# A two-layer hybrid trunk: the mixer's tiles in two pools, stores issued by ScalarE, another first order of gate and up

## The chip, the cores and the metric

The kernel runs on one core of one Trainium2 chip. The metric is the device time of one execution in microseconds (us). Before the change it is 2234.05 us, the median of 3 runs (2232.53 to 2235.14). TensorE (PE) multiplies, VectorE (DVE), ScalarE (ACT) and GpSimd (POOL) work on tiles, SyncE (SP) issues most of the loads. Each engine takes its own instructions in order; a DMA is issued by an engine and then runs beside it.

## The reference

Two layers of a transformer-like trunk on 256 tokens of width 2048, all in float32. Cut to what matters here:

```python
for l in range(2):
    h = rms_norm(x, pre_mix_norm[l])
    m = hybrid_mixer(h, ...)            # h @ w_in, two kinds of attention, @ w_o
    x = x + rms_norm(m, post_mix_norm[l])
    h = rms_norm(x, pre_ffn_norm[l])
    f = (silu(h @ w_gate[l]) * (h @ w_up[l])) @ w_down[l]      # 2048 -> 5632 -> 2048
    x = x + rms_norm(f, post_ffn_norm[l])
```

The mixer has 8 heads of stick-breaking attention and 8 of differential attention; each head's output is normed, and all are multiplied by `w_o`.

## The kernel before, in words

**Weights.** All weights pass through the core once, in the order that `weight_order` (L49) writes out, as tiles of 256 rows x 512 columns, stored as 128 partitions x 2 x 512 (512 KB). A tile's number is its place in that order. Of a layer's 392 tiles 96 belong to `w_in`, 32 to `w_o`, 176 to gate and up, taken in turn, and 88 to `w_down`. Gate and up of layer 0 begin at tile 128. `kp` (0 to 7) counts the pairs of 128 rows, `c` (0 to 10) the chunks of 512 columns of gate and up.

Each ordinary tile is loaded by SP into `raw` (`fetch`, L150, with the load in L165; four buffers), and split in two parts for the fp32r multiplier: ScalarE writes the rounded `hi`, VectorE the rest `lo = raw - hi` (`feed`, L202; L212 and L214 in the profile; six buffers each). Each product is three matmuls, hi x hi, lo x hi and hi x lo (`product`, L750; L754 to L756 in gate and up, L397 to L399 in the projections). `weights(i, ahead)` lets loads and splits run `LOOKAHEAD` tiles ahead of the matmuls.

**Combined products.** For some `kp` (`sevens`) the 2 x 2 block product of two token halves and the gate and up tiles is made with seven products in place of eight (`seven`, L871, `seven_products`, L771). That needs, besides the gate tile, the sum of up and gate. `summed` (L170) makes it without an engine's arithmetic: SP loads the up tile into `T` (L173), then POOL issues a second DMA that adds the first half of the gate tile to it (L174). The gate tile itself comes as `G` (L161). `fetch` issues `T` up to `EARLY` = 4 tiles ahead of its turn. `mixed_weights` (L179) then splits `T` into `hi` and `lo` (L188 and L189), forms three more tiles from `T` and `G`, and splits these into `Th` and `Tl`. At the end of the last combined `kp` of a chunk, `shared_part` (L788) reads four banks and writes four tiles `w`, with VectorE's last steps in L794 and L795; these release TensorE's banks. The token sums for a combined `kp` (`pair_sums`, L854) are made by VectorE and ScalarE ahead of their use.

In chunk 0 of each layer the order of `kp` is `FIRST_ORDER` (L38), the combined ones are `FIRST_SEVEN` = (4, 6), and `FORM_AT` (L39) says at which place in the order, counted after the first two, which `kp` gets its token sums. In the other chunks the order is 0 to 7 and the combined ones are 2, 4, 5 and 6. So in chunk 0 of layer 0 tiles 128 to 135 are `kp` 0, 1, 3 and 2; before the change 136 and 137 are `kp` 4, the first combined one (`G136`, `T137`).

**Pools.** Every pool is a stretch of on-chip memory, tiles of one `tag` share a ring of buffers, and a new tile waits until the tiles whose room it takes are no longer used. The mixer's tiles (`x`, `mix`, `t2`, `qk`, `v`, `gpost`, the attention weights, `ra`, `rb`) lie in one pool `att{l}` (L800) in the order of their first use. After the mixer it is released, and the FFN's pools `ffn{l}` (L847) and `gu{l}` (L848; `G` with 3 buffers, `T` with 4, `Th`, `Tl`) take the same stretch. The tag `t2` is also that of the squares that the FFN's norm throws away (`inv_rms`, L356). `mix{l}_{k}`, the mixer's normed output, has 16 buffers, made at the start of the layer and written by `norm_pair` (L434).

**From the mixer to the FFN.** Around the last chunk of `w_o` ScalarE's and VectorE's order is written out by hand (`tc.manual_schedule`). `rescale` (L417) adds the normed output to `x`, `transposed` (L330) turns `x` into `xF`, the stationary tiles of the FFN, with ScalarE (L338) and VectorE (L343), `inv_rms` computes the norm's factors for both halves of the tokens, and `put_away` (L245) stores the four quarters of `x` (512 KB each) to DRAM, from which they come back at the end of the FFN. It is called three times: after the mixer of each layer, and at the end of layer 0's FFN, twelve stores in all. Before the change POOL issues them (L250).

The compiler's scheduler places the instructions of each engine; DMAs are tracked by a limited number of completion semaphores (lanes), which the queues of an engine's kind take in turn, so that an issue may have to wait until an earlier transfer on its lane has landed.

Of the kernel before, what the change touches and what calls it, by code (L numbers as in the profile page):

```python
# [9 lines left out]
F32 = mybir.dt.float32  # L10
F32R = mybir.dt.float32r
# [6 lines left out]
P = 128  # L18
D = 2048
S = 256  # L20
L = 2
NT = S // P
KT = D // P
NH = 8
# [10 lines left out]
KP_O = (4, 5, 6, 7, 0, 1, 2, 3)  # L35
SEVEN = (2, 4, 5, 6)
FIRST_SEVEN = (4, 6)
FIRST_ORDER = (0, 1, 3, 2, 4, 5, 6, 7)  # L38
FORM_AT = {1: 4, 3: 6, 4: 5, 5: 2}  # L39
DOWN_SEVEN = (3, 6, 9, 12, 15, 18)  # L40

WARM = 13
# [9 lines left out]
def weight_order():  # L52

    order = []

    def queue_pair(name, l, kp, c):
        order.append((name, l, kp, c))
        return len(order) - 1

    plan = []  # L60
    sevens = set()
    for l in range(L):
        lay = {"in": {}, "o": {}, "gate": {}, "up": {}, "down": {}}
        chunks = []
        for g in range(2):
            chunks += [6 + g, 8 + g, 10 + g]
        for g in range(2):
            chunks += [g, 2 + g, 4 + g]
        lay["chunks"] = chunks
        for c in chunks:  # L70
            for kp in range(KT // 2):
                lay["in"][c, kp] = queue_pair("w_in", l, kp, c)
        order_o = [(c, kp) for kp in KP_O for c in (0, 1)]
        order_o += [(c, kp) for c in (2, 3) for kp in range(KT // 2)]
        lay["order_o"] = order_o
        for c, kp in order_o:
            lay["o"][c, kp] = queue_pair("w_o", l, kp, c)
        for c in range(FF // CW):
            for kp in FIRST_ORDER if c == 0 else range(KT // 2):
                lay["gate"][c, kp] = queue_pair("w_gate", l, kp, c)  # L80
                lay["up"][c, kp] = queue_pair("w_up", l, kp, c)
                if kp in (FIRST_SEVEN if c == 0 else SEVEN):
                    sevens.add(lay["up"][c, kp])
        for half in range(2):
            for kp in range(FF // P // 2):
                for c in (2 * half, 2 * half + 1):
                    lay["down"][c, kp] = queue_pair("w_down", l, kp, c)
                if kp in DOWN_SEVEN:
                    sevens.add(lay["down"][2 * half + 1, kp])
        plan.append(lay)  # L90
    return order, plan, sevens


def weights_laid_out(inputs):

    import numpy as np

    order = weight_order()[0]
    out = np.empty((len(order), P, 2 * CW), np.float32)
    for o, (name, l, kp, c) in zip(out, order):  # L100
        w = inputs[name][l, kp * 2 * P : (kp + 1) * 2 * P, c * CW : (c + 1) * CW]
        o[...] = w.reshape(2, P, CW).transpose(1, 0, 2).reshape(P, 2 * CW)
    return out


@with_exitstack
def kernel(
# [15 lines left out]
    nc = tc.nc  # L123
# [8 lines left out]
    def bank(name):  # L132
        return ps.tile([P, CW], F32, tag="b", bufs=3, name=name)
# [84 lines left out]
    def in_turn():  # L218

        return tc.issue_after(loads[-1].ins)  # L220
# [10 lines left out]
    xs = []  # L231
# [3 lines left out]
    away = []  # L235
# [9 lines left out]
    def put_away(nm):  # L245

        away.append(kept.tile([P, NT, D], F32, name=f"away_{nm}"))
        for t in range(NT):
            for h in range(2):
                nc.gpsimd.dma_start(away[-1][:, t, h * D // 2 : (h + 1) * D // 2], xs[t][h])  # L250

    x_pool = [None]

# [63 lines left out]
    def rsqrt(dst, src, inv, nm):  # L317
        n = dst.shape[-1]
        m = small.tile([P, 2, 4], F32, tag="rsq", bufs=4, name=f"rsq_{nm}")
        u, ms = m[:, 0, 0:n], m[:, 1, 0:n]  # L320
        nc.scalar.activation(u, src, AF.Ln, scale=inv, bias=eps)
        nc.scalar.activation(dst, u, AF.Exp, scale=-0.5)
        nc.vector.tensor_scalar(out=ms, in0=src, scalar1=inv, scalar2=EPS, op0=ALU.mult, op1=ALU.add)
        nc.vector.tensor_tensor(out=u, in0=dst, in1=dst, op=ALU.mult)
        nc.vector.tensor_tensor(out=u, in0=u, in1=ms, op=ALU.mult)
        nc.vector.tensor_scalar(out=u, in0=u, scalar1=-0.5, scalar2=1.5, op0=ALU.mult, op1=ALU.add)
        nc.vector.tensor_tensor(out=dst, in0=dst, in1=u, op=ALU.mult)
# [106 lines left out]
    def norm_pair(pool, ob, mix, mixed, h0, gcol, nm):  # L434
        ss = small.tile([P, 4], F32, tag="oss", name=f"oss_{nm}")
        for i in range(4):
            junk = pool.tile([P, CW], F32, tag="t2", name=f"jo_{nm}_{i}")
            nc.scalar.activation(junk[:, 0:P], ob[:, i * P : (i + 1) * P], AF.Square, accum_out=ss[:, i : i + 1])
        yield
        rs = small.tile([P, 4], F32, tag="ors", name=f"ors_{nm}")  # L440
        rsqrt(rs, ss, 1.0 / P, nm)
        on = pool.tile([P, 4, P], F32, tag="t2", name=f"on_{nm}")
        nc.vector.tensor_tensor(
            out=on, in0=ob.rearrange("p (i d) -> p i d", i=4), in1=rs.unsqueeze(2).to_broadcast([P, 4, P]), op=ALU.mult
        )
        yield
        yield
        pb = bank(f"oT_ps_{nm}")
        for i in range(4):
            nc.tensor.transpose(pb[:, i * P : (i + 1) * P], on[:, i, :], ident)  # L450
        for j in range(2):
            nc.scalar.activation(
                mix[h0 + j][:, 0, :], pb[:, j * S : (j + 1) * S], AF.Copy, scale=gains[:, gcol + j : gcol + j + 1]
            )
            nc.vector.scalar_tensor_tensor(
                out=mix[h0 + j][:, 1, :],
                in0=pb[:, j * S : (j + 1) * S],
                scalar=gains[:, gcol + j : gcol + j + 1],
                in1=mix[h0 + j][:, 0, :].bitcast(F32),
                op0=ALU.mult,  # L460
                op1=ALU.subtract,
            )
            mixed.add(h0 + j)
# [141 lines left out]

    def rotate(pool, tok, t, nm):
        v16 = tok.rearrange("p (h d) -> p h d", d=64)[:, :, 0:16]
        ra = pool.tile([P, NH, 16], F32, tag="ra", bufs=2, name=f"ra_{nm}")
        rb = pool.tile([P, NH, 16], F32, tag="rb", bufs=2, name=f"rb_{nm}")

        def table(a, b):
            return rope_sb[:, t, a:b].unsqueeze(1).to_broadcast([P, NH, b - a])

        eng = nc.gpsimd
        eng.tensor_tensor(out=ra, in0=v16, in1=table(0, 16), op=ALU.mult)
        eng.tensor_tensor(out=rb[:, :, 0:8], in0=v16[:, :, 8:16], in1=table(16, 24), op=ALU.mult)
        eng.tensor_tensor(out=rb[:, :, 8:16], in0=v16[:, :, 0:8], in1=table(24, 32), op=ALU.mult)
        eng.tensor_tensor(out=v16, in0=ra, in1=rb, op=ALU.add)
# [123 lines left out]
            else:  # L742
                evac()

    def load_gain(pool, v, nm):
        gp = pool.tile([P, D], F32, tag="gpost", bufs=1, name=f"gpost_{nm}")
        with in_turn():
            nc.sync.dma_start(gp, v.partition_broadcast(P))
        return gp
# [47 lines left out]
    xT = None  # L797
    for l in range(L):

        pool = tc.alloc_tile_pool(name=f"att{l}", bufs=6, reuse_waits="tile")  # L800
        if l == 0:
            xT = x_tiles("xT0")
            rs = []
        xs[:] = [[pool.tile([P, D // 2], F32, tag="x", bufs=4, name=f"x{l}_{t}_{h}") for h in range(2)] for t in range(NT)]
        mix = [pool.tile([P, 2, S], F32R, tag="mix", bufs=KT, name=f"mix{l}_{k}") for k in range(KT)]
        mixed = set()
        mixer_in(pool, l, rs, xT, mix, mixed)

        gpost = load_gain(pool, post_mix_norm[l], f"mix{l}")
        mg = {}  # L810
        ssm = [small.tile([P, 4], F32, tag="ssm", name=f"ssm_o{l}_{t}") for t in range(NT)]
        accs = {(c, t): acc_bank(f"o{l}_{c}_{t}") for c in (0, 1) for t in range(NT)}
# [34 lines left out]
        pool = tc.alloc_tile_pool(name=f"ffn{l}", bufs=5, reuse_waits="tile")  # L847
# [6 lines left out]
        def pair_sums(kp):  # L854
            f = pool.tile([P, 2, S], F32, tag="t2", name=f"f{l}_{kp}")
            for kk in range(2):
                st = xT[2 * kp + kk]
                nc.vector.tensor_tensor(out=f[:, kk, :], in0=st[:, 0, :].bitcast(F32), in1=st[:, 1, :].bitcast(F32), op=ALU.add)
            forms[kp] = token_sums(pool, gu, len(SEVEN), f[:, 0, 0:P], f[:, 1, 0:P], f[:, 0, P:S], f[:, 1, P:S], f"{l}_{kp}")
# [18 lines left out]
        for c in range(FF // CW):  # L878
            banks = four_banks(c % 2, [f"c{q}_{l}_{c}" for q in ("11", "12", "21", "22")])
            mine = FIRST_SEVEN if c == 0 else SEVEN  # L880
            order = FIRST_ORDER if c == 0 else tuple(range(KT // 2))
            if c == 0:
# [5 lines left out]
            for n, kp in enumerate(order):  # L888
                if c == 0 and n in FORM_AT:
                    pair_sums(FORM_AT[n])  # L890
                if kp not in mine:
# [32 lines left out]
        gpost = load_gain(dn, post_ffn_norm[l], f"ffn{l}")  # L924
# [151 lines left out]
```

## Time and profile before

| | |
|---|---|
| median of 3 runs | 2234.05 us (2232.53 to 2235.14) |
| the profiled execution's own time | 2232.69 us |
| its span, first to last instruction | 2230.9 us |
| PE granted clock, mean | 0.994 |
| DMA | 464.65 MB, mean 208 GB/s |
| SP's `raw` loads, issue to landing, median | 4.3 us |
| POOL's additions into `T`, the same | 6.7 us |
| POOL's stores `away_ffn`, the same | 3.7 us |

A row of the timeline has the start, the length in us, the engine, the line, the operation and its tiles; the bracket at its end holds the idle time of that engine just before and what ended it. Matmul ends are modelled, so the pace of matmuls is read from their starts. PE, PEld (its weight loads), DVE, ACT and POOL are the engines; SPq, POOLq and ACTq are the issues of DMAs. A row "DMA" in the chain is the transfer itself, from issue to landing. The granted clock is the share of TensorE's full speed in a stretch.

### The profile page before, as it was taken

How to read it: one execution, taken by the hardware profiler on the slowest of the kernel's cores; microseconds unless marked ns; L12 is line 12 of the kernel's file. 1: busy time of each engine (PE TensorE's matmuls, PEld its weight loads, DVE VectorE, ACT ScalarE, POOL GpSimd, SP SyncE). 2: the span in 40 equal slices, each digit the busy share in tenths (PEclk: the TensorE clock that was granted, in tenths of full speed). 3: DMA queues.
4: the chain of work that ended last, by engine and by line, in shares of the span. 5: the costliest groups of instructions: out<-in, count | busy, mean ns of one | idle time of the engine just before them, and what ended most of it. 6: DMA issues, size and time to landing. Idle time of an engine off the chain costs nothing.

```text
span 2230.9 us, 28481 instructions
## 1 busy us (share of the span) xinstructions
PE 2197.5 (99%) x10057; PEld 1805.2 (81%) x10057; DVE 1789.6 (80%) x2531; ACT 1308.2 (59%) x1937; POOL 139.8 (6%) x196
## 2 busy tenths in 40 slices
PE   9999999899999999999999999998999999999998
PEld 7888888688888888788877888887888888888886
DVE  6666555799999998989776665557999999999897
ACT  6555554656656656656565455546566566566663
POOL 1100000100000000000020000001000000000000
PEclk9999999999999999999999999999999999999999
DMA  8555555677776675767465554557767767757673
GB/s 289 190 168 163 160 189 183 224 228 233 217 253 213 218 249 184 239 214 241 153 224 171 179 189 160 183 187 229 248 215 225 242 212 228 239 194 245 198 254 100
DMA packets 136784, 464.65 MB, mean 208 GB/s; under 512 B 15681, under 2 KB 16193, under 8 KB 136129
## 3 DMA queue, kind: packets, MB, share of 16 engines
q1 hardware_dynamic: 119216, 428.20, 55.7%
q0 software_dynamic: 17280, 34.61, 8.5%
q8 instruction: 79, 1.29, 0.2%
q14 instruction: 65, 0.52, 0.1%
q10 hardware_dynamic: 144, 0.02, 0.0%
HBM read 454.38 MB, written 8.39 MB: 207 GB/s over the span
## 4 chain that ended last, share of the span: by engine, by line
PE 92%; DMA 3%; ACT 2%; DVE 2%; issue 1%; POOL 0%; SPq 0%; DVEq 0%; ACTq 0%; POOLq 0%
PE c L754 9%; PE c L756 9%; PE c L755 9%; PE in L397 7%; PE in L399 7%; PE in L398 7%; PE dn L960 5%; PE dn L963 5%; PE dn L961 5%; PE o L399 2%; PE o L398 2%; PE o L397 2%; PE p L754 2%; PE p L756 2%; PE p L755 2%; DMA raw<-in_weights_in_turn_dram 2%
## 5 line engine op out<-in xcount | busy, mean ns | idle before, releaser
L214 DVE TENSOR_TENSOR lo<-raw,hi 128x1024 fp32r<-128x1024 f32 x567 | 688.3, 1225 | 237.5 <-ACT hi L212 233.7
L212 ACT ACTIVATE hi<-raw 128x1024 fp32r<-128x1024 f32 x567 | 592.4, 1056 | 389.8 <-PE in L399 167.3
L754 PE MATMUL c<-hi,xF 128*128 128x512 f32 x820 | 324.3, 397 | 1.9 <-DVE w L795 1.6
L756 PE MATMUL c<-hi,xF 128*128 128x512 f32 x820 | 320.3, 391 | 0.0
L755 PE MATMUL c<-lo,xF 128*128 128x512 f32 x820 | 319.7, 390 | 0.0
L754 PEld LDWEIGHTS c<-hi,xF 128*128 128x128 f32 x820 | 155.1, 189 | 34.5 <-DVE w L795 2.5
L756 PEld LDWEIGHTS c<-hi,xF 128*128 128x128 f32 x820 | 154.3, 188 | 32.6
L960 PE MATMUL dn<-hi,jh 128*128 128x512 f32 x464 | 180.7, 389 | 0.0
L961 PE MATMUL dn<-lo,jh 128*128 128x512 f32 x464 | 180.5, 389 | 0.0
L755 PEld LDWEIGHTS c<-lo,xF 128*128 128x128 f32 x820 | 154.8, 189 | 30.9
L174 POOL DMA_DIRECT2D T<-in_weights_in_turn_dram x108 | 95.0, 880 | 1151.9 <-DMA T<-in_weights_in_turn_dram 476.4
L214 DVE TENSOR_TENSOR lo<-G,hi 128x1024 fp32r<-128x1024 f32 x108 | 131.6, 1219 | 33.4 <-ACT hi L212 33.3
L397 PE MATMUL in<-hi,xI 128*128 128x512 f32 x384 | 154.0, 401 | 0.2 <-ACT xI L338 0.2
L397 PE MATMUL in<-hi,xT 128*128 128x512 f32 x384 | 153.7, 401 | 0.0
L399 PE MATMUL in<-hi,xI 128*128 128x512 f32 x384 | 150.3, 391 | 0.3 <-DVE xI L343 0.3
L398 PE MATMUL in<-lo,xI 128*128 128x512 f32 x384 | 149.9, 390 | 0.5 <-DVE lo L214 0.5
L399 PE MATMUL in<-hi,xT 128*128 128x512 f32 x384 | 150.1, 391 | 0.0
L398 PE MATMUL in<-lo,xT 128*128 128x512 f32 x384 | 149.7, 390 | 0.4 <-DVE lo L214 0.4
L189 DVE TENSOR_TENSOR lo<-T,hi 128x1024 fp32r<-128x1024 f32 x108 | 131.6, 1219 | 21.4 <-ACT hi L188 20.9
L188 ACT ACTIVATE hi<-T 128x1024 fp32r<-128x1024 f32 x108 | 113.4, 1050 | 54.6 <-PE c L756 26.5
L963 PE MATMUL dn<-hi,jl 128*128 128x512 f32 x464 | 142.9, 389 | 0.0
L189 DVE TENSOR_TENSOR Tl<-G,Th 128x1024 fp32r<-128x1024 f32 x108 | 131.6, 1218 | 8.3 <-ACT Th L188 8.3
(306 smaller groups left out, 4272.5 us busy)
## 6 DMA issues: line engine op xcount, KB each, us to landing
raw<-in_weights_in_turn_dram SPq DMA_DIRECT2D x567, 512.0 KB, 4.3
T<-in_weights_in_turn_dram SPq DMA_DIRECT2D x108, 512.0 KB, 4.3
G<-in_weights_in_turn_dram SPq DMA_DIRECT2D x108, 512.0 KB, 4.5
T<-in_weights_in_turn_dram POOLq DMA_DIRECT2D x108, 256.0 KB, 6.7
away_ffn<-x POOLq DMA_DIRECT2D x8, 512.0 KB, 3.7
xd<-away_ffn SPq DMA_DIRECT2D x8, 512.0 KB, 10.1
xr<-in_x_columns_dram SPq DMA_DIRECT2D x8, 256.0 KB, 6.4
x<-in_x_dram SPq DMA_DIRECT2D x4, 512.0 KB, 8.8
```

Of the source, the lines that this page charges most:

```text
L189: nc.vector.tensor_tensor(out=l, in0=w, in1=h.bitcast(F32), op=ALU.subtract)
L212: nc.scalar.activation(hi, raw, AF.Copy)
L214: nc.vector.tensor_tensor(out=lo, in0=raw, in1=hi.bitcast(F32), op=ALU.subtract)
L397: nc.tensor.matmul(a, sh, hi[:, kk, :], start=first and kk == 0, stop=False)
L398: nc.tensor.matmul(a, sh, lo[:, kk, :], start=False, stop=False)
L399: nc.tensor.matmul(a, sl, hi[:, kk, :], start=False, stop=last and kk == 1)
L754: nc.tensor.matmul(a, sh, hi, start=first, stop=False)
L755: nc.tensor.matmul(a, sh, lo, start=False, stop=False)
L756: nc.tensor.matmul(a, sl, hi, start=False, stop=last)
L960: nc.tensor.matmul(accs[c, t], sh, hi[:, kk, :], start=first, stop=False)
L961: nc.tensor.matmul(accs[c, t], sh, lo[:, kk, :], start=False, stop=False)
L963: nc.tensor.matmul(accs[c, t], sl, hi[:, kk, :], start=False, stop=last)
```

## The change

- `Rooms` puts the mixer's tiles in two pools instead of one: `lasting` (tags `gpost`, `t2`, `x`, `qk`) and `passing` (all others: `mix`, `v`, the attention weights, `ra`, `rb` and so on). `lasting` is allocated first, and its tile `gpost` is made first of all, ahead of its load.
- The `mix` tiles are made when `norm_pair` writes them, two at a time, and no longer at the start of the layer.
- `ra` and `rb`, scratch tiles of the rotary step on POOL, have one buffer each instead of two.
- The twelve stores of `put_away` are issued by ScalarE instead of POOL.
- In chunk 0 of gate and up `kp` 7 comes before the first combined `kp` (4), and `kp` 5 after the last (6). So in layer 0 tiles 136 and 137 are the ordinary `kp` 7, and the first combined tiles are `G138` and `T139`, then `G140` and `T141`. The token sums of `kp` 6 are made one place earlier.

```diff
-FIRST_ORDER = (0, 1, 3, 2, 4, 5, 6, 7)
-FORM_AT = {1: 4, 3: 6, 4: 5, 5: 2}
+FIRST_ORDER = (0, 1, 3, 2, 7, 4, 6, 5)
+FORM_AT = {1: 4, 2: 6, 4: 5, 5: 2}
...
+class Rooms:
+    LASTING = ("gpost", "t2", "x", "qk")
+
+    def __init__(self, tc, name):
+        self.lasting = tc.alloc_tile_pool(name=f"{name}_lasting", bufs=6, reuse_waits="tile")
+        self.passing = tc.alloc_tile_pool(name=f"{name}_passing", bufs=6, reuse_waits="tile")
+
+    def tile(self, *args, **kw):
+        return (self.lasting if kw["tag"] in self.LASTING else self.passing).tile(*args, **kw)
+
+    def release(self):
+        self.passing.release()
+        self.lasting.release()
...
-                nc.gpsimd.dma_start(away[-1][:, t, h * D // 2 : (h + 1) * D // 2], xs[t][h])
+                nc.scalar.dma_start(away[-1][:, t, h * D // 2 : (h + 1) * D // 2], xs[t][h])
...
+        for j in range(2):
+            mix[h0 + j] = pool.tile([P, 2, S], F32R, tag="mix", bufs=KT, name=f"mix_{nm}_{j}")
         pb = bank(f"oT_ps_{nm}")
...
-        ra = pool.tile([P, NH, 16], F32, tag="ra", bufs=2, name=f"ra_{nm}")
-        rb = pool.tile([P, NH, 16], F32, tag="rb", bufs=2, name=f"rb_{nm}")
+        ra = pool.tile([P, NH, 16], F32, tag="ra", bufs=1, name=f"ra_{nm}")
+        rb = pool.tile([P, NH, 16], F32, tag="rb", bufs=1, name=f"rb_{nm}")
...
-    def load_gain(pool, v, nm):
-        gp = pool.tile([P, D], F32, tag="gpost", bufs=1, name=f"gpost_{nm}")
+    def load_gain(pool, v, nm, gp=None):
+        if gp is None:
+            gp = pool.tile([P, D], F32, tag="gpost", bufs=1, name=f"gpost_{nm}")
...
-        pool = tc.alloc_tile_pool(name=f"att{l}", bufs=6, reuse_waits="tile")
+        pool = Rooms(tc, f"att{l}")
+        gpost = pool.tile([P, D], F32, tag="gpost", bufs=1, name=f"gpost_mix{l}")
...
-        mix = [pool.tile([P, 2, S], F32R, tag="mix", bufs=KT, name=f"mix{l}_{k}") for k in range(KT)]
-        mixed = set()
+        mix, mixed = {}, set()
         mixer_in(pool, l, rs, xT, mix, mixed)
 
-        gpost = load_gain(pool, post_mix_norm[l], f"mix{l}")
+        load_gain(pool, post_mix_norm[l], f"mix{l}", gpost)
```

## The prediction

> **What bounds the kernel now.** I read the page first, then busy time by stretches, then TensorE's own timeline where its row thins out, then what each stop waited for.
>
> ```profile
> span 2230.9 us, 28481 instructions
> PE 2197.5 (99%) x10057; PEld 1805.2 (81%) x10057; DVE 1789.6 (80%) x2531; ACT 1308.2 (59%) x1937; POOL 139.8 (6%) x196
> ```
>
> TensorE is the bound almost everywhere; only 33 us of the span are not PE. The question is where those lie. The stretches below are the first chunk and a half of gate and up in each layer (406 to 506 and 1517 to 1615); the columns are the length, the busy time of PE, PEld, DVE, ACT and POOL, then the granted clock, the DMA share and GB/s.
>
> ```profile
> 406.00:429.00 23.00, 22.60 (x107) 18.22 (x105) 21.55 (x74) 16.58 (x52) 1.07 (x2) 1.00 0.66 239
> 429.00:439.00 10.00, 2.75 (x7) 1.47 (x8) 3.04 (x6) 3.26 (x4) 2.70 (x3) 0.73 1.05 323
> 439.00:506.00 67.00, 65.59 (x282) 53.23 (x281) 62.67 (x79) 41.82 (x48) 6.13 (x7) 0.96 0.76 235
> 1517.00:1540.00 23.00, 22.03 (x104) 17.79 (x102) 21.52 (x75) 16.01 (x50) 1.84 (x3) 1.00 0.68 242
> 1540.00:1548.00 8.00, 2.85 (x7) 1.51 (x7) 2.08 (x4) 2.84 (x4) 1.87 (x3) 0.68 1.06 339
> 1548.00:1615.00 67.00, 65.94 (x282) 53.54 (x283) 62.98 (x79) 42.21 (x48) 6.15 (x7) 0.96 0.77 236
> ```
>
> In 429 to 439 all engines stand still together, the DMA engines are full (1.05), and the granted clock falls to 0.73. The same happens in layer 1. TensorE's timeline shows the price; the brackets hold the idle time and what ended it.
>
> ```profile
> 428.14 0.39 PE L755 MATMUL c<-lo,xF 128*128 128x512 f32 x1
> 428.37 0.39 PE L756 MATMUL c<-hi,xF 128*128 128x512 f32 x1
> 431.54 0.50 PE L754 MATMUL p<-hi,xF 128*128 128x512 f32 x1 [2.79 <-ACT hi L212]
> 431.88 0.39 PE L754 MATMUL c<-hi,xF 128*128 128x512 f32 x1
> 432.80 0.50 PE L755 MATMUL p<-lo,xF 128*128 128x512 f32 x1 [0.53 <-DVE lo L214]
> ...
> 433.62 0.63 PE L756 MATMUL c<-hi,xF 128*128 128x512 f32 x1
> 438.43 0.80 PE L754 MATMUL q<-hi,sh 128*128 128x512 f32 x1 [4.18 <-ACT hi L188]
> ...
> 442.95 0.63 PE L756 MATMUL c<-hi,xF 128*128 128x512 f32 x1
> ...
> 443.81 0.40 PE L755 MATMUL c<-lo,xF 128*128 128x512 f32 x1
> ```
>
> At full clock a matmul starts every 0.23 us (428.14 to 428.37). Beyond that pace the three stops cost 2.94, 0.69 and 4.58 us; then matmuls come every 0.43 us from 438.43 to 443.81, 5.4 us at half speed, 2.5 us lost. Together 10.7 us. In layer 1 the brackets below are 2.31, 0.53 and 3.12; with the same small additions 2.5, 0.7 and 3.5 us, and some 3 at half speed: 9.7 us.
>
> ```profile
> 1541.50 0.50 PE L754 MATMUL p<-hi,xF 128*128 128x512 f32 x1 [2.31 <-ACT hi L212]
> ...
> 1542.76 0.69 PE L755 MATMUL p<-lo,xF 128*128 128x512 f32 x1 [0.53 <-DVE lo L214]
> ...
> 1547.85 0.79 PE L754 MATMUL q<-hi,sh 128*128 128x512 f32 x1 [3.12 <-ACT hi L188]
> ```
>
> The chain that ended last names the cause: the added tile T is loaded, then added to by a second transfer from POOL, then converted.
>
> ```profile
> 422.70 6.40 DMA T<-in_weights_in_turn_dram
> ...
> 429.72 7.58 DMA T<-in_weights_in_turn_dram
> 437.32 1.06 ACT hi L188
> ```
>
> **What the change does to that.** *The tile's room.* Before, the first T lies where the mixer's t2 tiles lay, and t2 is written by the squares of the FFN's own norm; so on SP it stands behind four raw loads, of which the last two wait for weight tiles that are converted late. In the changed kernel's built order the first two T loads stand right behind raw134 and raw135, and their rooms are those of attention weights, dead since the mixer. In the trace raw134 and raw135 go out at 403.9 and 406.0.
>
> ```profile
> L165 SPq DMA_DIRECT2D raw<-in_weights_in_turn_dram x2: 328/328/328, 403.9 to 406.0; - x2
> ```
>
> So the first T is issued at 404.2 (403.9 + 0.33) instead of 422.7. With the two transfers at their crowded price, the 14.6 us from 422.70 to 437.30 (429.72 + 7.58), it is whole at 418.8. *The first order* puts one ordinary pair of rows (kp 7) before the first combined product: 24 matmuls of 0.23 us, 5.4 us, so by my walk (below) T is wanted only at about 435. The margin is 16 us. G has a margin of its own: by the walk issued about 410 and wanted at 427, and it needs no add. The matmuls are the same in number; this step by itself costs nothing.
>
> **What is late next: VectorE.** Its busy time in 406 to 506 is 21.55 + 3.04 + 62.67 = 87.3 us, idle 12.7. The changed order gives it the same instructions up to the last of chunk 1's shared sums (L795), which TensorE must await for its next banks:
>
> ```profile
> 495.11 7.05 DMA raw<-in_weights_in_turn_dram
> ...
> 503.35 1.23 DVE lo L214
> 504.57 0.60 DVE w L794
> 505.17 0.61 DVE w L795
> ...
> 505.82 0.50 PE c L754
> ```
>
> So TensorE's 10.7 us are worth only what VectorE's own timeline shortens. Its idle time there, by releaser:
>
> ```profile
> DVE lo L189 <- ACT hi L188: 5.1, 1, 5.1
> DVE lo L214 <- ACT hi L212: 4.4, 2, 2.5
> DVE Tl L189 <- ACT Th L188: 1.7, 3, 0.9
> DVE xF L343 <- ACT xF L338: 1.4, 2, 1.2
> ```
>
> (The figures are all idle time in the window, how many times, the longest.) The 5.1 and 1.9 of the 4.4 are the stall. The other 2.5 is the raw load of 495.11, late in the ring of four, and stays. Up to 468, a point well inside chunk 1, VectorE idles 9.3 us before: 5.1 + 1.9 + 1.4 + 0.9. I walked the new order by hand with the pitches of the trace (a 1024-wide lo 1.14 us, a 512-wide step 0.60, a hi 1.0).
>
> ```profile
> 438.41 1.23 DVE L189 TENSOR_TENSOR lo<-T,hi 128x1024 fp32r<-128x1024 f32 x1 [5.06 <-ACT hi L188]
> 439.55 1.22 DVE L214 TENSOR_TENSOR lo<-raw,hi 128x1024 fp32r<-128x1024 f32 x1
> ...
> 417.29 2.02 ACT L212 ACTIVATE hi<-raw 128x1024 fp32r<-128x1024 f32 x2
> ```
>
> New idle appears in two places. First, ScalarE now converts tiles 134 and 135 (at 417.29 before) after the whole norm: the last four scalings, a square, two stores, Ln and Exp come first, so I put hi134 at 422.4 to 423.5. TensorE wants it at about 423.1 and waits some 0.9 us in two pieces; VectorE idles 3.0 us there in five pieces, against 1.4. Second, one sum's low part waits 0.6 to 1.5 us behind a converted raw tile, as the raw ring of four is still DMA-paced. Together about 3.8, against 9.3: **5.5 us won in layer 0**. Layer 1 idles 11.4 us (1.48 + 5.92 + 4.02) against 12.7, about half a microsecond less of it in the removed part: **5.0 us**. Later chunks have no TensorE wait before, so the gain is kept to the end.
>
> **The other edits.** *Stores by ScalarE*: each of twelve loses 0.54 us on POOL, which is idle, and takes an issue on ScalarE.
>
> ```profile
> 0.84 0.39 ACTq L268 DMA_DIRECT2D gains<-in_gain_columns_dram  x1
> L250 POOL DMA_DIRECT2D away_ffn<-x x8: 531/535/744, 401.7 to 1530.6; - x8
> ```
>
> A small load from ScalarE took 0.39 us of its queue; I take that for a store. The eight of the two FFN starts are in the walk. The four at the end of a layer stand behind work on the same data, and TensorE is released there by VectorE, not ScalarE. I take 0, bounds −0.5 (an x half is added earlier) and +1.6 (4 × 0.39). *Stores share the completion lanes of SP's loads*: four loads and three stores get a wait on each other, with 4 us margin by the walk. *ra and rb in one buffer*: POOL runs them one after another anyway; 0, bound +0.2. *gpost first, mix tiles late, x and qk apart*: the built order shows no later release in the mixer; 0.
>
> The sum: 2232.69 (span 2230.9 and 1.8 around it) − 5.5 − 5.0 = 2222.2 for a run like the profiled one, which lies 1.36 below the median. For a median I say **2223.5**.
>
> The half clock follows a stop of 4.8 us (433.62 to 438.43). The 0.96 of 439 to 506 is that half clock (4.8 us at half make 0.036 of 67) and nothing else, so the short wait for w at 505.82 left the clock alone. [...]
>
> **The rivals.**
> *The whole stall is won.* If VectorE's new waits are smaller than walked and TensorE never waits for it, the gain is 10.7 + 9.7 = 20.4: 2213.6. For it: VectorE's work, 87.3 us, would fit. Against: it would have to run with hardly any idle time, through ScalarE's order and the raw ring.
> *The late conversions cost more.* If hi134 to hi137 come 3 us later than walked (twelve loads between 404 and 414, 6 MB, are 19 us at the 323 GB/s of the full stretch), VectorE loses those 3 us in each layer: gain 4.5, 2229.5.
> *The tiles come no earlier*, because the new T or G still waits for something live: 2234. Against it: their waits in the built order are on attention work and the last w_o product.
> *Slower: a store holds ScalarE.* The last store stands ahead of hi134 and waits for the landing of G's load. Landing after 421.9 moves hi134, and so everything, one for one. The gain is gone when it lands near 427.4, 17 us after issue, and 3 us beyond that in each layer give 2240. Against it: in the old burst of seven the slowest took 12.8 us.
>
> ```profile
> 426.23 0.46 SPq L173 DMA_DIRECT2D T<-in_weights_in_turn_dram  x1
> 439.45 0.86 POOL L174 DMA_DIRECT2D T<-in_weights_in_turn_dram  x1 [3.99 <-DMA T<-in_weights_in_turn_dram]
> ```
>
> Its add at 439.45 followed the landing at 439.02. [...]
>
> **How the numbers follow.** Forecast (2219 to 2229) 0.60; whole stall (2213 to 2219) 0.16; late conversions (2229 to 2231) 0.11; no earlier tiles (about 2234) 0.06; slower 0.07. A measurement of this kernel tells about 0.2%, 4.5 us, from no change. Faster by more: the first two and about half of the third, 0.82; within: the rest of the third and the fourth, 0.11; slower: 0.07. The range from 2213 to 2230 leaves out the last two cases and the edges.
>
> **What would show it.** T's first load at about 404 and its add landed before 420; no stop of TensorE over 1.5 us in 420 to 440 and granted clock 1.00; waits of TensorE for VectorE (Tl, lo, w) spread over chunk 1, some 5 us in all per layer; VectorE busy near 93% from 423 on; w L795 at about 500.3. I am wrong if TensorE waits for hi134 or hi135 over 3 us, if the clock still falls, or if chunk 1 shows no waits for VectorE.

## The result

The changed kernel takes 2221.9 us (median of 6 runs, 2220.65 to 2224.29) against 2233.94 us before (6 runs, 2231.73 to 2235.76): ratio 0.9949, 95% interval 0.9936 to 0.9961, so 12.0 us less. The forecast was 10.5 us less, 2223.5. The profiled execution of the changed kernel took 2224.29 us, the highest of its six (span 2222.6), and lies 8.4 us below the one of before; the two profiles therefore show less than the medians do. Its mean granted clock is 0.997, that of the other five 0.998 or 0.999, so they spent less time at half clock than it did.

### The profile after

The stretches of before, in the changed kernel (length, busy time of PE, PEld, DVE, ACT, POOL, granted clock, DMA share, GB/s):

```profile
406.00:429.00 23.00, 21.98 (x105) 17.40 (x104) 20.22 (x59) 20.18 (x55) 2.74 (x3) 1.00 1.03 346
429.00:439.00 10.00, 10.00 (x46) 8.26 (x44) 10.00 (x20) 6.88 (x8) 0.89 (x1) 1.00 0.82 285
439.00:506.00 67.00, 63.96 (x284) 51.45 (x283) 63.46 (x87) 38.97 (x47) 5.19 (x6) 1.00 0.72 220
1517.00:1540.00 23.00, 22.21 (x101) 17.76 (x100) 20.83 (x52) 17.63 (x37) 1.75 (x2) 1.00 0.99 320
1540.00:1548.00 8.00, 8.00 (x37) 6.38 (x36) 8.00 (x13) 4.68 (x6) 0.85 (x1) 1.00 0.74 217
1548.00:1615.00 67.00, 63.61 (x278) 51.10 (x277) 62.09 (x85) 38.93 (x47) 4.31 (x5) 0.97 0.68 213
```

The hole of 429 to 439 is gone: TensorE and VectorE are both busy for all 10 us, and the DMA engines are full before 429 instead of after. TensorE now loses time in 439 to 506 and 1548 to 1615, in which before it lost little outside the half clock. The issues of SP and POOL say why the hole is gone:

```profile
404.14 0.33 SPq L182 DMA_DIRECT2D raw<-in_weights_in_turn_dram  x1
404.52 0.42 SPq L190 DMA_DIRECT2D T<-in_weights_in_turn_dram  x1
409.46 1.01 POOL L191 DMA_DIRECT2D T<-in_weights_in_turn_dram  x1 [273.78 <-ACT hi L229]
```

T is issued at 404.52 (422.70 before), and its addition, 8.3 us from issue to landing, is down at 417.7 (437.3 before). TensorE's timeline holds these stops of over half a microsecond in layer 0, and the longest of layer 1:

```profile
424.28 0.74 PE L774 MATMUL c<-hi,xF 128*128 128x512 f32 x2 [0.57 <-ACT hi L229]
455.21 0.50 PE L774 MATMUL c<-hi,xF 128*128 128x512 f32 x1 [0.94 <-DVE w L813]
470.66 0.73 PE L774 MATMUL p<-Th,sh 128*128 128x512 f32 x2 [1.01 <-ACT Th L205]
500.38 0.50 PE L774 MATMUL c<-hi,xF 128*128 128x512 f32 x1 [1.08 <-DVE w L815]
...
1600.77 0.39 PE L774 MATMUL c<-hi,xF 128*128 128x512 f32 x1
1602.98 0.64 PE L774 MATMUL c<-hi,xF 128*128 128x512 f32 x1 [1.83 <-DVE w L815]
1603.42 0.63 PE L775 MATMUL c<-lo,xF 128*128 128x512 f32 x1
```

None is longer than 1.5 us in layer 0, from start to start. Of the four, two end on VectorE (`w`) and two on ScalarE (`hi`, `Th`). In layer 1 a stop of 2.2 us (1600.77 to 1602.98) is followed by 3.4 us at half clock (granted clock 0.50 from 1603.19): the matmuls after 1602.98 start every 0.43 us. The `w` of that stop stands on VectorE behind a raw tile that took 7.03 us to land:

```profile
1592.30 7.03 DMA raw<-in_weights_in_turn_dram
...
1602.33 0.61 DVE w L815
```

Since every kernel of the table issues the same 10057 matmuls, the start of the n-th in two traces can be subtracted. The table gives, against before, what each stretch won (minus) or lost in the profiled executions:

| kernel | opening, mixer 0 | gate and up 0 | down 0 to mixer 1 | gate and up 1 | down 1 | sum |
|---|---|---|---|---|---|---|
| full change | +0.3 | −5.9 | −2.3 | −2.2 | +2.0 | −8.1 |
| rooms_alone | +0.5 | −4.7 | −2.1 | −3.1 | +0.2 | −9.2 |
| order_alone | 0.0 | −1.9 | −2.0 | +2.2 | −0.1 | −1.8 |
| stores_alone | +0.8 | −1.1 | −1.4 | +1.6 | 0.0 | −0.2 |
| rooms_stores | −0.1 | −2.8 | −2.9 | +1.7 | +1.0 | −3.1 |
| rooms_order | −0.2 | −8.7 | −2.3 | −7.3 | +1.5 | −17.0 |

(Bounds at matmuls 1800, 3900, 6800 and 8900.) In the down columns sits a stop at the first combined product of a down projection that comes and goes: 2.2 us in layer 0 of before and none in layer 1, 0.75 and 2.2 us in the changed kernel. It is in one layer or the other of kernels whose code there is the same, so I put none of it down to the change; no run tests that. Without it the full change won 8.5 us in this profile: 5.9, 2.2, and 0.7 at the layer boundary, less 0.3 in the opening.

### The profile page after: what moved, and what is told of

Its sections match the earlier page's. It is cut to its first block, busy times and chain, and to the rows that moved or that the text cites. A ratio compares the mean times of both kernels' runs of the same rounds, so it can differ in the third digit from the quotient of the medians.

```text
span 2222.6 us, 28460 instructions
## 1 busy us (share of the span) xinstructions
PE 2197.2 (99%) x10057; PEld 1803.2 (81%) x10057; DVE 1790.0 (81%) x2531; ACT 1307.7 (59%) x1937; POOL 135.1 (6%) x184
## 4 chain that ended last, share of the span: by engine, by line
PE 87%; DVE 7%; issue 2%; DMA 2%; ACT 2%; SPq 0%; DVEq 0%; ACTq 0%
PE c L774 8%; PE c L775 8%; PE c L776 8%; PE in L414 8%; PE in L416 8%; PE in L415 8%; PE dn L980 5%; PE dn L981 5%; PE dn L983 5%; PE o L416 3%; PE o L415 3%; PE o L414 2%; PE p L775 2%; PE p L774 2%; PE p L776 2%
## 5 line engine op out<-in xcount | busy, mean ns | idle before, releaser
L205 ACT ACTIVATE Th<-T 128x512 fp32r<-128x512 f32 x108 | 67.7, 627 | 127.5 <-DVE T L210 127.1
```

## The experiments

Twelve kernels were run. Times are medians; the ratio is to the kernel before on the same chip, with its 95% interval.

### Which part of the change does it

**rooms_alone**: before, with `Rooms`, the late mix tiles, the early `gpost`, and single `ra` and `rb`.

```diff
-        pool = tc.alloc_tile_pool(name=f"att{l}", bufs=6, reuse_waits="tile")
+        pool = Rooms(tc, f"att{l}")
...
```

> The two pools, late mix tiles, single ra and rb, on the kernel before; stores by POOL and the old first order. If the tile's room is what ended the stall (my theory), the first T is issued at about 404, whole by 420, well ahead of its use at 428, and the time is that of the full change, 2221 to 2225. If the first order is needed as well (rival: the split of T and G comes too late for a use at 428, since ScalarE is in the norm until 423), a stop of 2 to 4 us stays near 428 in each layer and the time is 2226 to 2230.

Measured: 2224.68 us, ratio 0.9962 (0.9949 to 0.9975). The first T goes out at 404.73 and its addition lands at 419.04. The stop near 428 is gone (one of 0.7 us is left at 430.9), so the edits to the room end it without the new order, and the rival is out. TensorE's longest stops are now at the ends of chunks 0 and 1, on VectorE, 2.45 and 2.13 us from start to start:

```profile
431.61 0.49 PE L774 MATMUL c<-Th,xF 128*128 128x512 f32 x1 [0.33 <-ACT Th L205]
...
454.26 0.50 PE L774 MATMUL c<-hi,xF 128*128 128x512 f32 x1 [2.07 <-DVE w L813]
...
501.74 0.50 PE L774 MATMUL c<-hi,xF 128*128 128x512 f32 x1 [1.75 <-DVE w L815]
```

**order_alone**: before, with the new first order.

```diff
+FIRST_ORDER = (0, 1, 3, 2, 7, 4, 6, 5)
+FORM_AT = {1: 4, 2: 6, 4: 5, 5: 2}
```

> The new first order and places of the token sums on the kernel before, nothing else. The first T still stands late in SP's queue, so it is whole near 437 and wanted 5.4 us later than before, near 434. My theory: of the stall of 10.7 us some 4 to 5 us stay, the clock may still fall, and after VectorE's catching up the gain is 2 to 4 us a layer: 2226 to 2230. The rival that the order alone ends the stall gives 2220 to 2224; the rival that it moves nothing gives 2234.

Measured: 2230.11 us, ratio 0.9985 (0.9976 to 0.9994), just outside my figure, on the slow side. T is issued at 422.9 and whole at 437.3 as before; wanted later, it still stops TensorE:

```profile
438.46 0.50 PE L754 MATMUL q<-hi,sh 128*128 128x512 f32 x1 [2.90 <-ACT hi L188]
439.72 0.80 PE L755 MATMUL q<-lo,sh 128*128 128x512 f32 x1 [0.76 <-DVE lo L189]
```

**rooms_order**: the full change with the stores back on POOL.

```diff
-                nc.scalar.dma_start(away[-1][:, t, h * D // 2 : (h + 1) * D // 2], xs[t][h])
+                nc.gpsimd.dma_start(away[-1][:, t, h * D // 2 : (h + 1) * D // 2], xs[t][h])
```

> The full change, but the twelve stores stay on POOL. My theory: stores on ScalarE are worth nothing, 2220 to 2224 and the same stops as in the full change. Rival (the stores on POOL hold the additions into T, or stores on ScalarE cost its queue): over 2 us from the full change either way, with the difference near 410 to 425.

Measured: 2214.89 us, ratio 0.9914 (0.9897 to 0.9930), below the interval of the full change. My expectation failed: the stores on ScalarE cost some 7 us, by the table 2.9 in gate and up of layer 0 and 5.1 in layer 1, of which 1.6 are the half clock after 1602.98, which rooms_order's trace does not have. This version beats both kernels.

**rooms_stores**: the full change with the old first order.

> The full change with the old first order. My theory: within 1.5 us of the two pools alone, whatever that gives; if the order is needed, slower than the full change by 4 to 8 us, as for the pools alone.

Measured: 2229.59 us, ratio 0.9982 (0.9972 to 0.9991): 4.9 us slower by the medians than rooms_alone on the same chip, with intervals that overlap slightly, so the stores cost here too, and my theory (within 1.5 us) fails. The old order costs 7.7 us against the full change, as in the second case.

**stores_alone**: before, with the stores by ScalarE.

> Only the stores by ScalarE, on the kernel before: old pools, old first order. By theory A it depends on whether the conversions of tiles 134 to 137 move behind the norm; if they do, the stop of TensorE that ends at 438 before comes on top of a new one near 424 and the time is 2236 to 2241; if T's load comes earlier for it, 2230 to 2234. The prediction's own step (stores worth nothing) gives 2232 to 2236.

Measured: 2231.51 us, ratio 0.9989 (0.9979 to 0.9998). The conversions do move behind the norm and two new stops appear (0.95 and 0.6 us at 424 to 426), but T's load also comes two places earlier on SP and the old stop shrinks, the second case of the expectation:

```profile
424.74 0.73 PE L754 MATMUL c<-hi,xF 128*128 128x512 f32 x2 [0.56 <-ACT hi L212]
...
433.60 0.50 PE L754 MATMUL p<-hi,xF 128*128 128x512 f32 x1 [2.63 <-ACT hi L212]
435.41 0.79 PE L755 MATMUL p<-lo,xF 128*128 128x512 f32 x1 [1.04 <-DVE lo L214]
```

So by the medians the stores win 3 us where T is late (it goes out at 420.72 instead of 422.70), and lose 5 to 7 where it isn't. Likewise the order wins 2.9 us alone and 9.8 beside the rooms. The parts don't add: rooms and order together win 18 us, alone 8.3 and 2.9. The clock has a share in that: the trace of rooms_alone has half clock after one such stop in each layer (from 455.15 and from 1605.44), some 1.6 us lost each time, and that of rooms_order has none.

### Why the stores on ScalarE cost

The place to look is ScalarE between 417 and 430. In rooms_order:

```profile
417.10 3.02 ACT L229 ACTIVATE hi<-raw 128x1024 fp32r<-128x1024 f32 x3
...
422.10 1.06 ACT L229 ACTIVATE hi<-raw 128x1024 fp32r<-128x1024 f32 x1
423.05 0.20 ACT L339 ACTIVATE rs_ffn<-rsq_ffn 128x1 f32<-128x1 f32 x1
423.14 1.06 ACT L229 ACTIVATE hi<-G 128x1024 fp32r<-128x1024 f32 x1
```

In the full change:

```profile
422.70 0.29 ACT L338 ACTIVATE rsq_ffn<-ssx_ffn,eps 128x1 f32<-128x1 f32 x1 [0.78 <-DVE ssx_ffn L379]
422.70 0.33 ACTq L267 DMA_DIRECT2D away_ffn<-x  x1
423.08 0.20 ACT L339 ACTIVATE rs_ffn<-rsq_ffn 128x1 f32<-128x1 f32 x1
423.19 3.89 ACT L229 ACTIVATE hi<-raw 128x1024 fp32r<-128x1024 f32 x4
426.98 1.04 ACT L229 ACTIVATE hi<-G 128x1024 fp32r<-128x1024 f32 x1
```

With the stores in its queue ScalarE finishes the norm and the stores first; tiles 134 to 137 (three of them done by 420.1 in rooms_order) wait for 423.19, and the first G for 426.98 instead of 423.14. VectorE idles 4.2 us in 406 to 470 (59.79 busy of 64) against 2.4 in rooms_order (61.64); of its waits on ScalarE there 1.4 us are for `sh`, 0.7 for the norm's factors and 0.2 for a `hi`, of which rooms_order has none. The two rows, rooms_order first:

```profile
406.00:470.00 64.00, 63.24 (x289) 51.65 (x288) 61.64 (x126) 45.64 (x85) 7.34 (x9) 1.00 0.81 274
406.00:470.00 64.00, 61.68 (x279) 49.06 (x277) 59.79 (x124) 46.62 (x87) 5.36 (x6) 1.00 0.80 259
```

Three experiments kept the stores on ScalarE and tried to give the conversions their place back.

**after_feed**: tiles 134 and 135 handed to the scheduler ahead of the norm.

```diff
+        feed(idx + 12)
         rs = [inv_rms(t, pool, f"ffn{l}") for t in range(NT)]
```

> The full change with the stores on ScalarE, but the conversions of tiles 134 and 135 (526 and 527 in layer 1) are given to the scheduler ahead of the FFN's norm, so that they stand before three of the four stores and most squares. Theory A: the stores on ScalarE cost 7 us only because they push these conversions from 417 to 423; then hi134 is back near 417 to 418, the stops of TensorE at 412 and 424 shrink to under 0.4 us, and the time is 2214 to 2217. Theory B: the issues on ScalarE, with their waits for landings of loads, cost by themselves: the time stays 2220 to 2223, and ScalarE idles ahead of a store.

Measured: 2224.81 us, ratio 0.9962 (0.9949 to 0.9975). hi134 is back at 416.78 and the stops at 424 are gone, but 136 and 137 still come at 424.49 and the first G at 426.39. Then a new wait appears: hi of tile 142 stands ahead of the token sums' `sh`, and both engines stand.

```profile
430.10 1.04 ACT L205 ACTIVATE hi<-T 128x1024 fp32r<-128x1024 f32 x1
434.58 1.06 ACT L229 ACTIVATE hi<-raw 128x1024 fp32r<-128x1024 f32 x1 [3.43 <-PE c L776]
435.54 0.61 ACT L786 ACTIVATE sh<-s 128x512 fp32r<-128x512 f32 x1
```

VectorE waits 2.97 us for that `sh` (its row at 436.19) and idles 6.1 us in 406 to 470. Theory A, as I put it (two conversions late), falls; the time lies just above theory B's figure too.

**after_urgent**: all four conversions at a priority above the norm.

```diff
+        with tc.high_priority(offset=URGENT):
+            feed(plan[l]["gate"][0, 7] + 2)
```

> The full change with its stores on ScalarE, but all four conversions of tiles 134 to 137 (526 to 529 in layer 1) are given a priority that puts them ahead of the second token half's norm, the stores of that half and Ln and Exp. after_feed moved only two of the four, and won nothing: the other two, and all that follow, were still at 424. Theory A2: the stores cost by the order of ScalarE's queue that they bring about (norm and stores ahead of the four conversions), so that G and T are converted 3 to 4 us late and VectorE, which is full, never recovers it; with the four ahead, hi of G138 comes near 423 and the time is 2214 to 2218. Theory B: the stores cost by themselves (issue time, waits for landings, their 2 MB beside the loads), wherever they stand: 2220 to 2224.

Measured: 2224.63 us, ratio 0.9962 (0.9950 to 0.9975). The four are done by 421.8, but now ScalarE stands at the norm's Ln, behind which the first G comes at 427.44:

```profile
425.10 0.29 ACT L338 ACTIVATE rsq_ffn<-ssx_ffn,eps 128x1 f32<-128x1 f32 x1 [2.45 <-DVE ssx_ffn L379]
...
427.44 1.04 ACT L229 ACTIVATE hi<-G 128x1024 fp32r<-128x1024 f32 x1
...
433.72 1.06 ACT L229 ACTIVATE hi<-raw 128x1024 fp32r<-128x1024 f32 x1 [2.39 <-PE c L776]
```

So theory A2's condition (G near 423) was not met, and the run can't decide between A2 and B. The time is above the figures of both.

**late80**: the stores at a lower priority.

```diff
-        put_away(f"ffn{l}")
+        with tc.high_priority(offset=-80):
+            put_away(f"ffn{l}")
```

> The full change with its stores on ScalarE, where the four stores of each FFN start are given a lower priority. In the built order hi134 then stands among the squares, hi135 to hi137 behind the last scalings and ahead of Ln, the last three stores behind them and ahead of hi of G138; Ln and Exp stand as in the version with stores on POOL (rooms_order). after_urgent left the question open: there hi of G138 came at 427.4 all the same, since ScalarE stood 2.4 us at Ln waiting for VectorE. Theory A3 (ScalarE's order alone costs; measure: the time at which G138 is converted, 423.1 at 2214.9, 426.4 to 427.4 at 2222 to 2225): hi of G138 before 424.5, VectorE idle under 3 us in 406 to 470, and 2214 to 2218. Theory B (the stores cost on ScalarE wherever they stand, by issue time and their waits): hi of G138 after 425.5, with ScalarE idle ahead of a store or of G138, and 2220 to 2225.

Measured: 2225.5 us, ratio 0.9963 (0.9949 to 0.9976), G at 425.61, VectorE idle 5.7 us in 406 to 470. Here a store's own price is seen:

```profile
424.00 0.20 ACT L339 ACTIVATE rs_ffn<-rsq_ffn 128x1 f32<-128x1 f32 x1
424.00 1.50 ACTq L267 DMA_DIRECT2D away_ffn<-x  x2
425.61 1.06 ACT L229 ACTIVATE hi<-G 128x1024 fp32r<-128x1024 f32 x1 [1.41 <-issue]
...
433.46 1.06 ACT L229 ACTIVATE hi<-raw 128x1024 fp32r<-128x1024 f32 x1 [3.43 <-PE c L776]
```

Two stores in a row take 1.50 us of the queue instead of 0.66 (two in a row took 0.81 in after_urgent), and G's conversion waits 1.41 us for them. That is by theory B; but the 3.43 us ahead of tile 142, with VectorE's wait for `sh`, are, as I read them, by order again. **What is settled**: moving the stores to ScalarE costs 5 to 7 us once T is early, and in every version that has them beside the rooms and the new order G is converted at 425.6 to 427.4 instead of 423.1 and VectorE idles 4.2 to 6.1 us instead of 2.4. **What stays open**: how it splits into the order and the issue; no run had rooms_order's order of ScalarE with the stores in it.

### What bounds the version without them

**ro_w**: rooms_order, shared sums at higher priority.

```diff
-                    shared_part(extra, w)
+                    with tc.high_priority(offset=URGENT):
+                        shared_part(extra, w)
```

> The two pools and the new order with the stores on POOL, and the shared sums w of each chunk of gate and up given a higher priority, so that on VectorE they stand ahead of the low parts of the last raw tiles. Theory: the stops of TensorE at the end of chunk 1 (2.5 us in layer 0, 2.4 in layer 1 in the version without it) are VectorE waiting in order for a raw tile that lands late, not VectorE's total work; then they vanish or fall under 0.5 us and the time is 2209 to 2212. Rival (VectorE's total work is the bound, the wait only moves on to the next tile): 2213 to 2217, with stops of the same sum elsewhere in chunks 1 and 2.

Measured: 2214.31 us, ratio 0.9912 (0.9897 to 0.9926): the same as rooms_order. The stops that it was aimed at (2.47 and 2.40 us) are gone, and others come in their place:

```profile
462.34 0.66 PE L934 MATMUL actT_ps<-ident,w 128*128 128x128 f32 x4 [1.71 <-DVE w L928]
470.39 0.73 PE L774 MATMUL p<-Th,sh 128*128 128x512 f32 x2 [0.56 <-ACT Th L205]
480.27 0.50 PE L774 MATMUL p<-Th,sh 128*128 128x512 f32 x1 [0.74 <-ACT Th L205]
```

In layer 1 fewer came, and gate and up 1 won 8.6 us against 7.3; the profiled execution was the slowest of its four (2217.84), so a gain under 2 us is possible and not shown. The rival has the better of it.

**ro_f**: rooms_order with the additions of `pair_sums` on POOL.

```diff
-                nc.vector.tensor_tensor(out=f[:, kk, :], ...)
+                nc.gpsimd.tensor_tensor(out=f[:, kk, :], ...)
```

> The two pools and the new order with the stores on POOL, and the sixteen additions of pair_sums (0.34 us each on VectorE) made by POOL. If VectorE's total work bounds chunks 0 and 1, 2.7 us less of it in each layer shorten TensorE's stops there by up to as much: 2209 to 2213. If the stops come from the order of VectorE's queue behind late raw tiles, nothing changes: 2213 to 2217. If POOL is slow enough to hold the token sums or the additions into T, a stop near 430 and over 2217.

Measured: 2228.41 us, ratio 0.9971 (0.9960 to 0.9983): the third case. An addition takes POOL 1.04 us (VectorE's own row in rooms_order has 0.42), VectorE waits 6.8 us for them, once in each layer, and TensorE stops 3.1 and 2.2 us at 437 to 442.

**ro_one** and **ro_one_w**: one combined product less in chunk 0, without and with ro_w's edit.

```diff
-FIRST_SEVEN = (4, 6)
-FORM_AT = {1: 4, 2: 6, 4: 5, 5: 2}
+FIRST_SEVEN = (6,)
+FORM_AT = {2: 6, 3: 4, 4: 5, 5: 2}
```

> The two pools and the new order with the stores on POOL, but chunk 0 of each layer has one combined product (kp 6) in place of two; kp 4 is done as an ordinary pair of tiles, its token sums one place later, since other chunks use them. TensorE gets 3 matmuls more in each layer (1.4 us in all), VectorE loses the forming of three tiles and the low part of Th there, about 3.6 us a layer. If VectorE's total work in chunks 0 and 1 is the bound that is left (as ro_w, which only changed its order, won nothing), TensorE's stops there (3.2 to 3.6 us a layer without it) mostly go: 2209 to 2213. If they come from late raw tiles, the time is 1.4 us longer or more: 2215 to 2219.

> ro_one and the higher priority of the shared sums of ro_w together. If VectorE's load and its order at the end of a chunk both count, the stops at the end of chunks 0 and 1 are under 0.5 us each and the time is 2206 to 2211, the lowest of all. If load alone counts, it equals ro_one within 1.5 us.

Measured: 2225.66 us, ratio 0.9962 (0.9950 to 0.9975), and 2223.47, ratio 0.9949 (0.9935 to 0.9963). Both are some 8 to 11 us slower than rooms_order, and my theory that VectorE's total is the bound falls with them. With less to do, VectorE idles 8.7 us in 406 to 470 instead of 2.4. ScalarE's waits in 406 to 460 (us in all, times, longest) point to the reason:

```profile
ACT hi L229 <- DMA raw<-in_weights_in_turn_dram: 11.4, 4, 5.3
ACT sh L786 <- DVE s L784: 5.1, 2, 3.1
ACT w L925 <- DVE w L924: 1.8, 1, 1.8
```

In rooms_order ScalarE waits 3.6 us for raw tiles in that stretch. Two tiles that came as G and T, loaded far ahead into rings of their own, now go through the raw ring of four, which is late already. As I read it, what is left is not one engine's load but the round of raw load, ScalarE and VectorE, each in order; no run changes the raw ring by itself.

## Why the prediction was right, and where it was wrong

- **The room and T.** Right. T went out 0.3 us later than forecast and was whole at 417.7 (forecast 418.8); rooms_alone shows that the edits to the room, taken together, end the stall by themselves. "The tiles come no earlier" is out.
- **VectorE next, half of the stall won.** Right for VectorE in layer 0: w L815 ends at 500.34 (forecast 500.3), 5.4 us earlier than before, and VectorE is busy 95% of 423 to 506 (forecast 93). TensorE's 5.9 us (forecast 5.5) are partly luck. In the built order it meets that wait for w 7 matmuls later than before, so it was not 5.4 but 7.0 us ahead there, and 1.4 were lost afterwards (below); the walk had neither. Its stops in 410 to 506 come to 5.3 us (start to start, less 0.23 us each), "some 5 us in all", but only 2.3 of them end on VectorE (`w`); the other 3.0 end on ScalarE (`Th` and `hi` 1.2 and 1.1, `xF` and `sh` the rest). "The whole stall is won" did not happen in the changed kernel; rooms_order comes near it (2214.9 for 2213.6).
- **Layer 1.** Forecast 5.0, in the profiled execution 2.2. The term that I left out is the clock: TensorE's wait for VectorE at the end of chunk 1 grew to 2.2 us, 3.41 us at half clock followed (granted clock 0.50 from 1603.19), and 8 matmuls lost 0.2 us each, 1.6 in all. The forecast has no half clock after the change. That was my estimate: the trace of before shows only that the wait for w at 505.82 (1.12 us) left the clock alone, and no run shows a length of stop up to which it stays whole. In the changed kernel it stayed whole in layer 0 (1.00 in 406 to 506) and not in layer 1. I had also misread the trace of before. "The half clock follows a stop of 4.8 us (433.62 to 438.43)", I wrote, but the granted clock fell at 433.58, ahead of that stop; before it lay the ends of two shorter ones, at 431.54 and 432.80:

```profile
430.16:433.58 3.42, 1.51 (x5) 0.97 (x6) 1.83 (x2) 1.58 (x2) 1.38 (x2) 1.00 1.02 410
433.58:436.99 3.41, 0.67 (x2) 0.00 (x0) 0.00 (x0) 0.00 (x0) 0.88 (x1) 0.50 1.06 273
```

- **"The gain is kept to the end."** Wrong by 1.4 us in layer 0 (6.97 us ahead at matmul 2400, 5.6 at 2800) and 1.8 in layer 1: through chunks 2 and 3 TensorE still waits a quarter microsecond at a time. Against it stand 0.7 us won at the layer boundary, in every kernel of the table with the stores on ScalarE and in none without; the bound of −0.5 that I set there was passed.
- **"Stores by ScalarE: I take 0."** This is the step that failed. The runs show 7 us (2214.9 without, 2221.9 with). The total came out since the walk had the price in it, unnamed: it took hi134 to 137 from the built order as late (422.4 to 423.5 forecast, 423.19 measured, TensorE's wait 0.9 forecast and 1.1 measured) and put that down to the norm. The order was the consequence of the stores, and a walk of the other order could have shown it. The rival of a store that holds ScalarE until G has landed did not occur: the last store went out at 422.70, when the first two loads of G had long landed (415.88 and 418.88), and ScalarE's wait just before it was for VectorE's sum (0.78 us).
- **"This step by itself costs nothing"**, of the first order: it costs nothing and wins 2.9 us alone, 9.8 beside the rooms. I had counted it only as margin for T. That it also spreads the combined products' work on ScalarE and VectorE is my reading; no run separates the two, and part of the 9.8 is the half clock of rooms_alone.
- **The sum.** 12.0 us measured, 10.5 forecast: two errors of opposite sign, 7 us of stores and about as much of order, lay in one built order and were walked together. That they cancel to 1.5 us is luck.

## What to carry to other kernels

A stall with every engine idle can be worth less than its length (in the changed kernel 5.9 of 10.7 us, in gate and up of layer 0): price what the next engine can give back, and walk the built order, not the diff. A change of several parts should be taken apart even when the total comes out, since a part that costs a third of what the others win (7 of 18 us here) can hide in it. Moving a cheap DMA issue to an engine that feeds the critical chain can cost more than the 0.33 us of the issue itself: look at where it and the work around it come to stand in that engine's order. Here the move cost 5 to 7 us, and how these split is open.

## What the runs showed of the hardware

Half clock came after some stops of TensorE and not after others. The stops are given from the start of one matmul to the start of the next, with the granted clock that followed:

| kernel | stop | length, us | granted clock after it |
|---|---|---|---|
| before | 428.37 to 431.54, then 431.88 to 432.80 | 3.17, 0.92 | 0.50 from 433.58, for 10.24 us |
| before | 1538.80 to 1541.50, then 1541.84 to 1542.76 | 2.70, 0.92 | 0.50 from 1542.91, for 10.24 us |
| before | 899.20 to 901.39 | 2.19 | 1.00 |
| full change | 1600.77 to 1602.98 | 2.21 | 0.50 from 1603.19, for 3.41 us |
| full change | 1998.01 to 2000.18 | 2.17 | 1.00 |
| rooms_order | 495.31 to 497.78 | 2.47 | 1.00 |

In these traces matmuls start every 0.23 us at a granted clock of 1.00 and every 0.43 us at 0.50. The length of one stop does not by itself tell which follows: 2.21 us was followed by half clock, 2.47 us was not. What else decides it no run here isolates.
